# One decoder layer on one core: the seven products of a pair on four PSUM banks

## The chip, the core and the metric

The kernel runs on one core of one Trainium2 chip, in one launch. The metric is the device time in microseconds (us) of that core, as the median of several executions. In the profile PE is TensorE (the matrix engine), DVE is VectorE, ACT is ScalarE, POOL is GpSimd and SP is the engine that issues most of the DMAs. SBUF is the on-chip memory that all engines work in, PSUM the eight banks of 512 fp32 values per partition into which PE accumulates its products. Each engine executes its own instructions in the order in which the program has them; between engines they wait on semaphores.

## The reference, cut to what matters

One layer with a sequence of 1024 and a model width of 1024, all in float32:

```python
xn = rmsnorm(x, norm_mix_w[l])
proj = xn @ w_in[l]                       # 1024 x 4352
...                                       # two attentions on parts of proj, gates, merge
x = x + merged @ w_mix_out[l]
xn = rmsnorm(x, norm_ffn_w[l])
u = xn @ w_up                             # 1024 x 5632
c = conv_b + sum over j of shifted u * conv_w[j]    # causal, width 3
gate, val = split(c)                      # 2816 columns each
x = x + (silu(gate) * val) @ w_down
```

The change lies in two of these products: part of `xn @ w_in` (the projection stage) and all of `xn @ w_up` (the hidden stage).

## The kernel before, in words

**Numbers.** Every fp32 matrix is held as a high and a low part in a reduced type (fp32r). A product of two such matrices takes three matmuls for each 128-row step of the contraction: high by high, high by low, low by high. Splitting is one copy on ACT (the high part) and one subtraction on DVE (the low part).

**Pairs.** The weight columns are taken in pairs of 128-column blocks, and each pair is multiplied by a Strassen-like scheme with seven block products in place of eight. The activations (transposed, 1024 channels by 1024 positions) are cut into quarters: by channels (first and second 512) and by positions (first and second 512). From these come the right-hand operands `B11`, `B21`, `B22` and the differences `T1` to `T4`, made once for a stage. From the weights of the pair come the left-hand operands `A11`, `A12`, `A22` and the sums `S1` to `S4`, made for each pair: `sum_pair` (lines 86 to 99) loads two blocks by DMA (`raw`, `rv`) and computes the sums on POOL (lines 96 to 99, tiles `sf`), `split_pair` (lines 102 to 115) splits them (ACT line 110, DVE line 112). The tiles have names and a few buffers each: `wh`/`wl` (2 buffers) take `A11` and `A12` together, then `A22`; `sh`/`sl` take `S1` and `S2` together, then `S3` and `S4` together (2 buffers in the projection, 3 in the hidden stage); `sf` has 2 buffers. A buffer is written again when its readers are done.

**The seven products.** `product` (line 828, matmuls on lines 835 to 837) puts one block product of 12 matmuls into one PSUM bank. `P1 = A11 B11`, `P2 = A12 B21`, `P3 = S4 B22`, `P4 = A22 T4`, `P5 = S1 T1`, `P6 = S2 T2`, `P7 = S3 T3`. Each has a bank of its own out of eight that rotate (pools `psA` and `psF`). `recombine` (lines 389 to 402) then makes the four quarters of the result: ACT copies `P1` to SBUF (`s1`, line 395); seven additions on DVE, each with one operand in PSUM, make `c11 = P2 + s1` (396), `u2 = P6 + s1` (397), `u3 = P7 + u2` (398), `c22 = P5 + u3` (399), `u4 = P5 + u2` (400), `c12 = P3 + u4` (401), `c21 = u3 - P4` (402). `c11` and `c12` are the two halves of the first block's tile `us`, `c21` and `c22` those of the second's.

**Behind it.** In the projection (nine pairs after five plain blocks) POOL multiplies each `us` by the row scale `rstd` (line 385) and `keep` (lines 404 to 420) splits it and stores it to DRAM. In the hidden stage (22 pairs, j = 0 to 21) `conv` (lines 962 to 973) follows for each `us`: multiplication by `rstd` on POOL (line 965), bias and first tap on ACT (line 970), two more taps on DVE (971, 972). `glu` (lines 950 to 959) applies SiLU on ACT (957), multiplies gate and value on DVE (958) and stores the result to DRAM. During one pair the operands of the next two are made.

**The first pair of the hidden stage.** The row scale is not ready when it starts. PE sums the squares (line 158), POOL raises them to the power -1/2 (line 167, tile `rs`), and PE spreads the result over the columns (eight transposes, line 173), from where ACT copies it into `rstd` (line 907). Before these eight transposes stand the first two products of pair 1.

**Order.** A tile framework turns the program into one instruction list for each engine and puts in the semaphores. The order within each list is fixed when the kernel is built. PE takes pair by pair, product by product; DVE, ACT and POOL each take a mix of three kinds of work: recombining this pair, the convolution of the pair before, the operands of the pairs to come.

Of the kernel before, what the change touches and what calls it, by code (L numbers as in the profile page):

```python
# [13 lines left out]
ALU = mybir.AluOpType  # L14
# [3 lines left out]
P = 128  # L18
# [4 lines left out]
H2 = 512  # L23
DFF = 2816
NF = DFF // P
# [17 lines left out]
class Trunk:  # L43
# [206 lines left out]
    def project(self):  # L250


        nc, tc = self.nc, self.tc
# [3 lines left out]
        with ExitStack() as ctx:  # L257
            e = ctx.enter_context
            psA = self.psT = e(tc.tile_pool(name="psA", bufs=8, space=PSUM, reuse_waits="tile"))
# [8 lines left out]
            bank = lambda: self.tl(psA, [P, H2], "t")  # L268
# [11 lines left out]
            def diffs(k):  # L280

                (a, a2), (b, b2) = ([xr[r][:, hf * H2:(hf + 1) * H2] for hf in range(2)] for r in (k, k + 4))
                tt = nc.vector.tensor_tensor
                tt(a, a2, a, ALU.subtract)
                tt(a2, b2, a2, ALU.subtract)
                tt(b2, b2, a, ALU.subtract)
                tt(b, b2, b, ALU.subtract)

            def parts(k):
                for n, r in enumerate((k, k + 4)):  # L290
# [81 lines left out]
                     ("P6", "S2", "T2"), ("P4", "A22", "T4"))  # L372
            for j, ms in enumerate(self.pairs):
                w = self.next_w()
                pp = {}
                for name, a, b in (prods[i] for i in ((0, 1, 4, 2, 3, 5, 6) if j == 0 else (0, 1, 2, 5, 3, 4, 6))):
                    pp[name] = bank()
                    self.product(pp[name], w[a], b)
                us = [self.tl(tp, [P, T], "us", bufs=3) for _ in range(2)]
                self.recombine(pp, us, tp, 0)  # L380
                for m, u in zip(ms, us):
                    if self.kind[m] == "g":
                        nc.sync.dma_start(self.gd[m - 18], u)
                    else:
                        nc.gpsimd.tensor_tensor(u, u, self.rstd, ALU.mult)
                        self.keep(m, u, (tp, "hi"))
        self.uw = None

    def recombine(self, ps, us, tp, o):

        nc = self.nc
        c11, c12, c21, c22 = (us[w][:, o + hf * H2:o + (hf + 1) * H2] for w in range(2) for hf in range(2))
        s1, u2, u3, u4 = (self.tl(tp, [P, H2], n, bufs=1) for n in ("s1", "u2", "u3", "u4"))
        tt = nc.vector.tensor_tensor
        nc.scalar.copy(s1, ps["P1"])
        tt(c11, ps["P2"], s1, ALU.add)
        tt(u2, ps["P6"], s1, ALU.add)
        tt(u3, ps["P7"], u2, ALU.add)
        tt(c22, ps["P5"], u3, ALU.add)
        tt(u4, ps["P5"], u2, ALU.add)  # L400
        tt(c12, ps["P3"], u4, ALU.add)
        tt(c21, u3, ps["P4"], ALU.subtract)

    def keep(self, m, u, to):

# [397 lines left out]
    def operands(self, xt, xtp, xw, k):  # L803

        tt = self.nc.vector.tensor_tensor
        (b11, b12), (b21, b22) = ([xw[kc][:, hf * H2:(hf + 1) * H2] for hf in range(2)] for kc in (k, k + 4))

        def put(name, t):
            hi, lo = self.split(xt[name, k, "h"], xt[name, k, "l"], t)
            if name == "T13":  # L810
                self.B["T1", k], self.B["T3", k] = ((hi[:, c], lo[:, c]) for c in (slice(0, H2), slice(H2, T)))
            else:
                self.B[name, k] = hi, lo

        put("B11", b11)
        put("B21", b21)
        put("B22", b22)
        if k == 3:
            self.t42.append(xw[k + 4])
        t4, t2 = (self.t42[k][:, c] for c in (slice(0, H2), slice(H2, T)))  # L820

        tt(b11, b12, b11, ALU.subtract)
        tt(b12, b22, b12, ALU.subtract)
        put("T13", xw[k])
        tt(t2, b22, b11, ALU.subtract)
        tt(t4, t2, b21, ALU.subtract)

    def product(self, ps, a, b, ks=range(4), first=True, last=True, skip=False):

# [9 lines left out]
    def hidden(self, pair):  # L839
        nc, tc = self.nc, self.tc  # L840
        with ExitStack() as ctx:
            e = ctx.enter_context
            psF = e(tc.tile_pool(name="psF", bufs=8, space=PSUM, reuse_waits="tile"))
            self.psT = psF
            xc2 = e(tc.tile_pool(name="xc2", bufs=1, side="right", reuse_waits="tile"))
            self.uw = e(tc.tile_pool(name="uw", bufs=3, side="right", reuse_waits="tile"))
            prods = (("P1", "A11", "B11"), ("P2", "A12", "B21"), ("P5", "S1", "T1"), ("P7", "S3", "T3"),
                     ("P3", "S4", "B22"), ("P6", "S2", "T2"), ("P4", "A22", "T4"))
            with tc.high_priority(400):
                w0 = self.split_pair(*pair)  # L850
            ready = {}
            for j in range(NF):
                w, ps = ready.pop(j) if j else (w0, {})
                if j == 0:

                    for name, a, b in prods[:5]:
                        ps[name] = self.tl(psF, [P, H2], "t")
                        self.product(ps[name], w[a], b, range(3), last=False)
                    for k in range(4):
                        hi, lo = self.split(*(xc2.tile([P, T], F32R, name=f"T42_{k}{p}") for p in "hl"), self.t42[k])  # L860
                        self.B["T4", k], self.B["T2", k] = ((hi[:, c], lo[:, c]) for c in (slice(0, H2), slice(H2, T)))
                    self.tctx.close()
                    tp = e(tc.tile_pool(name="tp", bufs=2, side="right", reuse_waits="tile"))
                    ssq = self.tl(psF, [P, H2], "t")
                    for n, (name, a, b) in enumerate(prods[:5]):
                        self.product(ps[name], w[a], b, (3,), first=False)
                        if n == 4:
                            self.col_sums(ssq, [self.rstd], NB, 0)
                            with tc.high_priority(400):
                                rs = self.rstd_cols(ssq, 8, D)  # L870
                if j == NF - 1:

                    with tc.high_priority(50):
                        for k, r in enumerate(raw):
                            for hf in range(2):
                                h = self.tl(self.uw, [P, 2, H2], ("sh", "sl", "rv", "rv", "sh", "sl")[2 * k + hf], F32R, **({"bufs": 2} if k == 1 else {}))
                                self.hs[hf, k] = self.split(h[:, 0], h[:, 1], r[:, hf * H2:(hf + 1) * H2])
                        lo = self.lo
                for name, a, b in (prods[i] for i in ((0, 1, 2, 5, 3, 6, 4) if j == NF - 1 else (0, 1, 2, 5, 3, 4, 6) if j else range(7))):
                    if name not in ps:  # L880
                        ps[name] = self.tl(psF, [P, H2], "t")
                        self.product(ps[name], w[a], b)
                us = [self.tl(tp, [P, T + 2], "us", bufs=3) for _ in range(2)]
                if j == NF - 1:
                    self.defer.pop(0)(lo)
                    self.xctx2.close()
                    self.uw = None
                    self.open_down()
                    self.deep = True
                    with tc.high_priority(100):  # L890
                        self.ahead(2)
                self.recombine(ps, us, tp, 2)
                if j < NF - 1:

                    w, ps = ready[j + 1] = self.next_w(), {}
                    if j == NF - 2:
                        raw = [self.tl(self.sfp[0], [P, T], "t42", bufs=1)] + [self.tl(self.sfp[0], [P, T], "sf") for _ in range(2)]
                        for k, r in enumerate(raw):
                            nc.sync.dma_start(r, self.hd[k])
                    for name, a, b in prods[:2 if j == 0 else 0]:  # L900
                        ps[name] = self.tl(psF, [P, H2], "t")
                        self.product(ps[name], w[a], b)
                if j == 0:
                    for hf in range(2):
                        sp = self.tl(psF, [P, H2], "t")
                        self.spread(sp, rs, hf * 4)
                        nc.scalar.copy(self.rstd[:, hf * H2:(hf + 1) * H2], sp)

                for w in range(2):
                    f = lambda after=None, j=j, w=w, us=us: self.glu(j, w, us[w], tp, after)  # L910
                    if j + w < NF - 1:
                        f()
                    else:
                        self.defer.append(f)
# [296 lines left out]
```

## Time and profile before

| what | value |
|---|---|
| median of 3 runs | 1356.11 us (1355.26 to 1356.71) |
| the profiled execution | 1356.2 us, of which the span from first to last instruction is 1354.3 us |
| granted PE clock, mean | 0.996 of full speed |
| matmuls recorded | 6304 |

The page of the profile gives each engine's busy time. A group line has an engine, an operation, the tiles written and read, a count and a mean duration. In a timeline each row has the start and the duration in us, then engine, source line, operation, tiles, shape, and in brackets for how long the engine had been idle before it and what ended that. PE's matmuls overlap in their pipeline, so the rate of PE is read from the distance between two starts and not from the duration of one.

### The profile page before, as it was taken

To read this page: it belongs to the slowest core of one execution; us is meant where nothing else is said; L and a number is where in the kernel's file an instruction comes from. 1 tells how busy PE (TensorE), PEld (TensorE's weight loads), DVE (VectorE), ACT (ScalarE), POOL (GpSimd) and SP (SyncE) were. 2 spreads that over 40 slices of the span, in tenths; PEclk is the share of its full clock that TensorE was granted. 3 is DMA by queue.
4 is the path that set the end of the run, shared out by engine and by line. 5 is a ranking of instruction groups with operands and counts; after the bars stand their busy time and mean duration, and the time that the engine had idled before them with its cause. 6 is when DMAs were issued, how large, how long until landed. Compare 5 with 4: busy or idle time off the path is not lost.

```text
span 1354.3 us, 17160 instructions
## 1 busy us (share of the span) xinstructions
PE 1335.0 (99%) x6304; PEld 1103.6 (81%) x6304; DVE 1009.8 (75%) x1454; ACT 603.9 (45%) x942; POOL 483.1 (36%) x350
## 2 busy tenths in 40 slices
PE   7999999999999999999999999999999999999997
PEld 6888888888887777878888888888888888888886
DVE  8846775388898875355689888888888898986454
ACT  8422232376667664334444334433443345433343
POOL 0436651010102125741455565555555611231011
PEclk9999999999999999999999999999999999999999
DMA  6334443966554235334422222122212248651342
GB/s 255 140 113 164 143 156 114 272 174 175 156 133 144 77 116 219 117 119 136 166 82 88 71 91 94 62 79 93 93 63 83 92 141 311 215 177 64 94 134 85
DMA packets 62470, 179.50 MB, mean 133 GB/s; under 512 B 6833, under 2 KB 15153, under 8 KB 62385
## 3 DMA queue, kind: packets, MB, share of 16 engines
q1 hardware_dynamic: 50928, 160.98, 36.7%
q10 hardware_dynamic: 11456, 17.41, 3.5%
q8 instruction: 50, 0.82, 0.2%
q14 instruction: 36, 0.29, 0.1%
HBM read 129.61 MB, written 48.76 MB: 132 GB/s over the span
## 4 chain that ended last, share of the span: by engine, by line
PE 62%; DVE 17%; POOL 7%; issue 7%; DMA 4%; ACT 3%; POOLq 0%; DVEq 0%; SPq 0%; ACTq 0%
PE t L836 7%; PE t L837 7%; PE t L835 7%; POOL us L965 3%; PE y L996 3%; PE d L996 3%; PE sc L568 3%; PE g L150 2%; PE g L151 2%; DVE c L958 2%; PE g L152 2%; DVE wl L112 2%; DMA gr<-gd 2%; PE sc L151 2%; PE sc L152 2%
## 5 line engine op out<-in xcount | busy, mean ns | idle before, releaser
L970 ACT ACTIVATE c<-us,vecs 128x1024 f32<-128x1024 f32 x44 | 54.8, 1248 | 163.2 <-POOL us L965 160.0
L965 POOL TENSOR_TENSOR us<-us,rstd 128x1024 f32<-128x1024 f32 x42 | 100.7, 2414 | 52.8 <-DVE wl L131 34.3
L110 ACT CAST sh<-sf 128x1024 fp32r<-128x1024 f32 x62 | 64.9, 1051 | 106.2 <-POOL sf L97 61.8
L129 ACT CAST wh<-raw 128x1024 fp32r<-128x1024 f32 (+2 forms) x60 | 60.7, 1012 | 104.8 <-PE sc L151 33.1
L971 DVE SCALAR_TENSOR_TENSOR c<-us,vecs,c 128x1024 f32<-128x1024 f32 x44 | 67.1, 1527 | 51.9 <-ACT c L970 51.9
L131 DVE TENSOR_TENSOR wl<-raw,wh 128x1024 fp32r<-128x1024 f32 (+2 forms) x60 | 75.3, 1256 | 39.1 <-ACT wh L129 29.3
L96 POOL TENSOR_TENSOR sf<-rv 128x512 f32<-128x512 f32 x30 | 42.5, 1417 | 166.7 <-DMA rv<-in_w_up 73.2
L112 DVE TENSOR_TENSOR sl<-sf,sh 128x1024 fp32r<-128x1024 f32 x62 | 88.3, 1426 | 8.2 <-ACT sh L110 8.2
L167 POOL TENSOR_TENSOR rs<-ms,mhalf 128x8 f32<-128x8 f32 (+2 forms) x9 | 14.5, 1614 | 159.1 <-DVE ms L165 148.5
L150 PE MATMUL g<-xh,wh 128*128 128x512 f32 x176 | 70.7, 402 | 0.1
L152 PE MATMUL g<-xh,wl 128*128 128x512 f32 x176 | 70.4, 400 | 0.0
L151 PE MATMUL g<-xl,wh 128*128 128x512 f32 x176 | 70.4, 400 | 0.0
L98 POOL TENSOR_TENSOR sf<-raw,rv 128x512 f32<-128x512 f32 x30 | 41.6, 1386 | 59.9 <-DVE sl L112 59.9
L572 DVE CUSTOM_DVE_ANT_0 L<-sc,bias 128x128 f32<-128x128 f32 (+7 forms) x64 | 47.7, 752 | 17.4 <-PE sc L568 14.1
L551 POOL MEMSET aT<- 128x128 f32 x32 | 6.1, 204 | 152.0 <-PE t L597 101.6
L573 ACT ACTIVATE L<-L,sm 128x128 f32<-128x128 f32 (+7 forms) x64 | 49.6, 778 | 20.7 <-DVE sm L572 18.2
L97 POOL TENSOR_TENSOR sf<-sf,raw 128x512 f32<-128x512 f32 x31 | 58.0, 1870 | 1.6
L972 DVE SCALAR_TENSOR_TENSOR c<-us,vecs,c 128x1024 f32<-128x1024 f32 x44 | 56.2, 1279 | 0.6
L725 POOL TENSOR_TENSOR gr<-gr,rstd 128x1024 f32<-128x1024 f32 x16 | 39.4, 2467 | 41.4 <-DMA gr<-gd 41.2
L112 DVE TENSOR_TENSOR wl<-raw,wh 128x1024 fp32r<-128x1024 f32 (+1 forms) x35 | 52.8, 1508 | 0.1
L151 PE MATMUL sc<-ml,wh 128*128 128x512 f32 x128 | 50.1, 391 | 0.6 <-DVE ml L746 0.6
L568 PE MATMUL sc<-u,u 128*128 128x512 f32 (+2 forms) x192 | 49.8, 359 | 0.1
(444 smaller groups left out, 4351.4 us busy)
## 6 DMA issues: line engine op xcount, KB each, us to landing
u<-qd SPq DMA_DIRECT2D x72, 256.0 KB, 6.1
raw<-in_w_down SPq DMA_DIRECT2D x27, 512.0 KB, 3.7
raw<-in_w_in SPq DMA_DIRECT2D x25, 512.0 KB, 4.4
hr<-hd SPq DMA_DIRECT2D x50, 256.0 KB, 5.3
raw<-in_w_up SPq DMA_DIRECT2D x23, 512.0 KB, 3.6
hd<-c SPq DMA_DIRECT2D x22, 512.0 KB, 2.8
rv<-in_w_up SPq DMA_DIRECT2D x21, 512.0 KB, 3.5
gr<-gd SPq DMA_DIRECT2D x16, 512.0 KB, 3.6
```

Of the source, the lines that this page charges most:

```text
L112: nc.vector.tensor_tensor(lo, src, hi.bitcast(F32), ALU.subtract)
L131: self.lo = (eng or nc.vector).tensor_tensor(wl, raw, wh.bitcast(F32), ALU.subtract)
L150: nc.tensor.matmul(ps, wh[:, kc + o, :], ah, start=first and n == 0, stop=False)
L151: nc.tensor.matmul(ps, wh[:, kc + o, :], al, start=False, stop=False)
L152: nc.tensor.matmul(ps, wl[:, kc + o, :], ah, start=False, stop=last and n == len(kcs) - 1)
L568: nc.tensor.matmul(sc[:, lo + n0:lo + n1], qs, k[c][part][:, n0:n1], start=part == 0, stop=part == 1)
L835: nc.tensor.matmul(ps, ah[:, k, :], bh, start=first and n == 0, stop=False, skip_group_check=skip)
L836: nc.tensor.matmul(ps, ah[:, k, :], bl, start=False, stop=False, skip_group_check=skip)
L837: nc.tensor.matmul(ps, al[:, k, :], bh, start=False, stop=last and n == len(ks) - 1, skip_group_check=skip)
L965: i = (nc.vector if m % NF == 0 else nc.gpsimd).tensor_tensor(us[:, 2:], us[:, 2:], self.rstd, ALU.mult)
L971: nc.vector.scalar_tensor_tensor(c, us[:, 1:T + 1], cw[1], c, ALU.mult, ALU.add)
L996: nc.tensor.matmul(ps, v[:, n, :], x, start=n == i == 0, stop=n == len(js) - 1 and i == 2)
```

## The change

The pairs after the first of each stage go through a new function, `seven`, with four PSUM banks in place of seven and the products in another order. Three products are accumulated onto a bank that already holds another one, once that one has been read: `P2` onto `P1`, `P4` onto `P7`, `P3` onto `P5`. For this the sign of `T4` is turned, so that `P4` is added.

```diff
-                tt(b, b2, b, ALU.subtract)
+                tt(b, b, b2, ALU.subtract)
...
                 us = [self.tl(tp, [P, T], "us", bufs=3) for _ in range(2)]
-                self.recombine(pp, us, tp, 0)
+                if j == 0:
+                    pp = {}
+                    for name, a, b in (prods[i] for i in (0, 1, 4, 2, 3, 5, 6)):
+                        pp[name] = bank()
+                        self.product(pp[name], w[a], b)
+                    self.recombine(pp, us, tp, 0)
+                else:
+                    self.seven(psA, w, us, tp, 0)
...
-        tt(c21, u3, ps["P4"], ALU.subtract)
+        tt(c21, ps["P4"], u3, ALU.add)
+
+    def seven(self, pool, w, us, tp, o):
+
+        nc = self.nc
+        c11, c12, c21, c22 = (us[r][:, o + hf * H2:o + (hf + 1) * H2] for r in range(2) for hf in range(2))
+        s1, u2, u3 = (self.tl(tp, [P, H2], n, bufs=1) for n in ("s1", "u2", "u3"))
+        tt = nc.vector.tensor_tensor
+        a, b, c, d = (self.tl(pool, [P, H2], "t") for _ in range(4))
+        self.product(a, w["A11"], "B11", skip=True)
+        nc.scalar.copy(s1, a)
+        self.product(b, w["S2"], "T2")
+        tt(u2, b, s1, ALU.add)
+        self.product(c, w["S3"], "T3", skip=True)
+        tt(u3, c, u2, ALU.add)
+        self.product(d, w["S1"], "T1", skip=True)
+        tt(c22, d, u3, ALU.add)
+        self.product(a, w["A12"], "B21", first=False, skip=True)
+        nc.scalar.copy(c11, a)
+        self.product(c, w["A22"], "T4", first=False, skip=True)
+        tt(c21, c, u2, ALU.add)
+        self.product(d, w["S4"], "B22", first=False, skip=True)
+        tt(c12, d, u2, ALU.add)
...
-        tt(t4, t2, b21, ALU.subtract)
+        tt(t4, b21, t2, ALU.subtract)
...
-                for name, a, b in (prods[i] for i in ((0, 1, 2, 5, 3, 6, 4) if j == NF - 1 else (0, 1, 2, 5, 3, 4, 6) if j else range(7))):
...
+                if j == 0:
+                    for name, a, b in prods:
+                        if name not in ps:
+                            ps[name] = self.tl(psF, [P, H2], "t")
+                            self.product(ps[name], w[a], b)
+                    self.recombine(ps, us, tp, 2)
+                else:
+                    self.seven(psF, w, us, tp, 2)
...
-                    for name, a, b in prods[:2 if j == 0 else 0]:
-                        ps[name] = self.tl(psF, [P, H2], "t")
-                        self.product(ps[name], w[a], b)
```

The last three removed lines are those that put the first two products of pair 1 ahead of the eight transposes in the hidden stage.

In the built kernel the matmuls of a pair stay 84. DVE loses two additions per pair (`c11` and `u4`), ACT gains one copy (`c11`). DVE's order in pair j of the hidden stage is: `u2`, gate times value of pair j-1, `u3`, `c22`, low part of `S3`/`S4` for pair j+1, low part of `A11`/`A12` for j+1, `c21`, low part of `A22` for j+1, `c12`, low part of `S1`/`S2` for j+2, and the four taps of the convolution of pair j; then `u2` of pair j+1. ACT's order is: `s1`, SiLU of j-1, high parts of `S3`/`S4` and of `A11`/`A12` for j+1, `c11`, high part of `A22` for j+1, high part of `S1`/`S2` for j+2, first taps of pair j (first block, then second). POOL's order is: the sums `S3`, `S4` for j+2, `us` of pair j times `rstd` (second block, then first), the sums `S1`, `S2` for j+3.

More of the change, by code (lines that the diff above doesn't have):

```diff
@@ L374, in project @@
                 w = self.next_w()
[L375 to L378, printed above, removed]
                 us = [self.tl(tp, [P, T], "us", bufs=3) for _ in range(2)]
-                self.recombine(pp, us, tp, 0)
+                if j == 0:
[6 more added lines that the diff above has]
+                    self.seven(psA, w, us, tp, 0)
                 for m, u in zip(ms, us):
@@ L878, in hidden @@
                         lo = self.lo
-                for name, a, b in (prods[i] for i in ((0, 1, 2, 5, 3, 6, 4) if j == NF - 1 else (0, 1, 2, 5, 3, 4, 6) if j else range(7))):
-                    if name not in ps:
-                        ps[name] = self.tl(psF, [P, H2], "t")
-                        self.product(ps[name], w[a], b)
                 us = [self.tl(tp, [P, T + 2], "us", bufs=3) for _ in range(2)]
+                if j == 0:
[6 more added lines that the diff above has]
+                    self.seven(psF, w, us, tp, 2)
                 if j == NF - 1:
@@ L891, in hidden @@
                         self.ahead(2)
-                self.recombine(ps, us, tp, 2)
                 if j < NF - 1:
@@ L899, in hidden @@
                             nc.sync.dma_start(r, self.hd[k])
-                    for name, a, b in prods[:2 if j == 0 else 0]:
-                        ps[name] = self.tl(psF, [P, H2], "t")
-                        self.product(ps[name], w[a], b)
                 if j == 0:
```

## The prediction

> **What bounds the kernel now.** I read the page first, then a table by stretches, then the timelines of four engines over one pair of the hidden stage.
>
> ```profile
> span 1354.3 us, 17160 instructions
> PE 1335.0 (99%) x6304; PEld 1103.6 (81%) x6304; DVE 1009.8 (75%) x1454; ACT 603.9 (45%) x942; POOL 483.1 (36%) x350
> ```
> ```profile
> core 0: us, PE busy (x) PEld busy (x) DVE busy (x) ACT busy (x) POOL busy (x), PEclk, DMA share, GB/s
> 726.20:1092.10 365.90, 365.57 (x1598) 298.65 (x1597) 313.32 (x304) 142.84 (x154) 205.09 (x151) 1.00 0.25 82
> 86.00:242.00 156.00, 156.00 (x690) 129.23 (x689) 106.31 (x109) 44.24 (x51) 76.86 (x46) 1.00 0.41 150
> 699.60:703.00 3.40, 3.40 (x9) 2.23 (x8) 3.40 (x4) 2.83 (x4) 0.10 (x1) 0.50 0.00 0
> ```
>
> PE is busy everywhere. The first stretch is pairs 2 to 20 of the hidden stage, with DVE at 313 of 366 us; the second is pairs 1 to 8 of the projection, with DVE at 106 of 156.
>
> ```profile
> 726.22 0.39 PE L835 MATMUL t<-B_0h,wh 128*128 128x512 f32 x1
> ...
> 840.55 0.39 PE L835 MATMUL t<-B_0h,wh 128*128 128x512 f32 x1
> 840.78 0.39 PE L836 MATMUL t<-B_0l,wh 128*128 128x512 f32 x1
> 841.23 0.51 PE L837 MATMUL t<-B_0h,wl 128*128 128x512 f32 x1
> ...
> 1092.03 0.39 PE L835 MATMUL t<-B_0h,wh 128*128 128x512 f32 x1
> ```
>
> Undisturbed matmuls start 0.227 us apart (840.55 to 840.78), so a product of 12 takes 2.72 and a pair of 84 takes 19.03. Pair 2 starts at 726.22 and pair 21 at 1092.03: 365.8 / 19 = 19.25 for a pair. The 0.22 more is one wait: at 841.23 PE comes 0.22 late, for the low part of `A11`. The next rows show who sets that.
>
> ```profile
> 839.30 1.88 DVE L112 TENSOR_TENSOR wl<-raw,wh 128x1024 fp32r<-128x1024 f32 x1
> 841.10 2.30 DVE L958 TENSOR_TENSOR c<-c,c 128x1024 f32<-128x1024 f32 x1
> ...
> 843.92 1.21 DVE L112 TENSOR_TENSOR sl<-sf,sh 128x1024 fp32r<-128x1024 f32 x1
> 845.05 0.68 DVE L398 TENSOR_TENSOR u<-t,u 128x512 f32<-128x512 f32 x1
> 845.77 0.69 DVE L399 TENSOR_TENSOR us<-t,u 128x512 f32<-128x512 f32 x1
> 846.38 0.68 DVE L400 TENSOR_TENSOR u<-t,u 128x512 f32<-128x512 f32 x1
> ...
> 847.77 1.22 DVE L112 TENSOR_TENSOR sl<-sf,sh 128x1024 fp32r<-128x1024 f32 x1
> ...
> 852.16 1.73 DVE L971 SCALAR_TENSOR_TENSOR c<-us,vecs,c 128x1024 f32<-128x1024 f32 x1 [2.58 <-ACT c L970]
> 853.80 0.68 DVE L112 TENSOR_TENSOR wl<-rv,wh 128x512 fp32r<-128x512 f32 x1
> 854.41 1.28 DVE L972 SCALAR_TENSOR_TENSOR c<-us,vecs,c 128x1024 f32<-128x1024 f32 x1
> 855.60 1.28 DVE L971 SCALAR_TENSOR_TENSOR c<-us,vecs,c 128x1024 f32<-128x1024 f32 x1
> ...
> 1091.81 1.21 DVE L958 TENSOR_TENSOR c<-c,c 128x1024 f32<-128x1024 f32 x1
> ```
> ```profile
> 838.80 1.29 POOL L96 TENSOR_TENSOR sf<-rv 128x512 f32<-128x512 f32 x1 [5.42 <-DVE c L972]
> ...
> 840.17 2.14 POOL L97 TENSOR_TENSOR sf<-sf,raw 128x512 f32<-128x512 f32 x1
> 845.21 1.29 POOL L98 TENSOR_TENSOR sf<-raw,rv 128x512 f32<-128x512 f32 x1 [2.90 <-DVE sl L112]
> 846.47 1.29 POOL L99 TENSOR_TENSOR sf<-raw,sf 128x512 f32<-128x512 f32 x1
> ...
> 847.93 4.87 POOL L965 TENSOR_TENSOR us<-us,rstd 128x1024 f32<-128x1024 f32 x2
> ...
> 1109.62 2.00 POOL L965 TENSOR_TENSOR us<-us,rstd 128x1024 f32<-128x1024 f32 x1 [4.47 <-DVE sl L756]
> ```
> ```profile
> 850.87 1.25 ACT L970 ACTIVATE c<-us,vecs 128x1024 f32<-128x1024 f32 x1 [7.48 <-POOL us L965]
> 852.03 0.60 ACT L110 CAST wh<-rv 128x512 fp32r<-128x512 f32 x1
> ...
> 853.99 0.56 ACT L395 COPY s<-t 128x512 f32<-128x512 f32 x1
> ...
> 857.62 1.04 ACT L110 CAST sh<-sf 128x1024 fp32r<-128x1024 f32 x1
> ```
>
> Two readings. First, a loop beside PE: `us` times `rstd` on POOL, first tap on ACT, taps on DVE, recombination on DVE, and again. None of these rows waits for PE. The recombination is a pair late, which eight rotating banks allow. Second, DVE and POOL exclude each other when DVE reads two SBUF tensors. Line 958 takes 1.21 alone (1091.81) and 2.30 where POOL's line 97 runs until 842.31. That one takes 2.14 against 1.29 of its sister at 846.47, because DVE's row from 839.30 ends at 841.18, 1.0 after its start. The two multiplications take 4.87 against twice 2.00, because DVE's row from 847.77 ends at 848.99. Who waits goes next. The additions at 845.05 to 846.38, with one operand in PSUM, keep their 0.68 beside POOL. So DVE work on SBUF and all POOL work form one queue.
>
> **The change part by part.** Two additions a pair leave DVE: at 0.61 from start to start (845.77 to 846.38) that is 1.2 us. DVE is not what PE waits for by its total, so this counts only inside the loop. The copy of `c11` on ACT (0.56 as at 853.99) lies in ACT's idle time. The sign and operand order of `T4` cost nothing: as many operations of the same shape, once a stage.
>
> The new wait. `T4`'s product goes onto `c` only when `u3` has read it; `u3` stands on DVE behind the whole convolution of the pair before, and behind the waiting matmul stands all of PE. Nominally that product starts 5 products, 13.6 us, into the pair. Before, the same lateness was covered by the spare banks. I follow the loop from the start of `u3` in pair j (time 0) in the order of the built program, with starts of successors from the rows above.
>
> `c22` at 0.7, low part of `S3`/`S4` 1.3 to 2.5. This frees `sf`, and POOL wants line 98 at 2.6. But DVE's next instruction, the low part of `A11`/`A12` (`A12`'s product, which held the buffer, is done), has begun at 2.45 and holds the path to 3.6; line 98 ends at 4.9. `c21` (after the product that started at about 0.75 and ended at 3.6) needs no path. The low part of `A22`, waiting since 4.3, goes next, to 5.5; line 99 ends at 6.75, a small fill comes behind it (846.47 to 847.93 is 0.17 more than the 1.29), and the multiplication of the second block runs to 8.9. PE ends the pair at about 6.3. `c12` follows to 7.05, the cast of `S1`/`S2` (their buffer is held by `S4` until then) ends at 7.45, and the low part behind it waits for POOL, 8.9 to 10.0. The first block's multiplication, kept back by that, ends at 12.0. First tap on ACT to 13.3. On DVE four taps at 1.2 each with POOL's line 97 (1.29) between them: 19.4. `u2` to 20.0, gate times value (1.15) to 21.1: there `u3` of pair j+1 starts. The loop is 21.1 us, and PE's 19.03 is shorter, so PE waits some 2 us in each pair at `T4`'s product.
>
> The full loop runs for j = 2 to 18, since POOL makes no more `S1`, `S2` after that: 17 x (21.1 - 19.25) = 31.5; pair 19 has the loop without lines 96 and 97, 19.8: 0.5. Together +32. Bounds for the loop: the four waits for the path (1.1, 0.6, 1.1, 1.3) are the part I only infer. With two of them gone it is 19.4, with none PE's 19.03; with one more POOL operation of 1.29 in the convolution 22.4. I take 21.1, as all four follow from who is queued first by margins of 0.15 to 0.6.
>
> The transposes.
>
> ```profile
> 696.59 1.95 PE L158 MATMUL t<-ones,rstd 128*128 128x1 f32 x16
> ...
> 706.26 0.39 PE L835 MATMUL t<-B_0h,wh 128*128 128x512 f32 x1
> ...
> 707.27 2.65 POOL L167 TENSOR_TENSOR rs<-ms,mhalf 128x8 f32<-128x8 f32 x1
> ...
> 708.98 0.39 PE L835 MATMUL t<-B_0h,wh 128*128 128x512 f32 x1
> ...
> 711.70 1.03 PE L173 MATMUL t<-ident,rs 128*128 128x128 f32 x8
> ...
> 712.49 0.48 PE L835 MATMUL t<-T_0h,sh 128*128 128x512 f32 x1
> ```
>
> Pair 1's first two products (706.26 to 711.70) covered the wait for `rs`, ready at 709.92. Without them PE is idle from 706.26 to 709.95: +3.7. Pair 1 then starts at 710.75. Its clock may fall: at 699.60 to 703.00 it was 0.50, after sixteen one-column matmuls, and 3.4 us held 9 matmuls where 15 fit. Such a stretch costs up to 1.7; I take 1.3, total +5.0 (3.7 to 5.4). The Trainium skill, TensorE: Matmul & The Clock Gate, section Why this matters for your kernels, tells to leave no PE-idle gaps of over about 3 us, or the clock halves. By it this gap would cost the 1.7, and the 2 us waits in the pairs nothing.
>
> The projection: DVE has 50 us idle there, and `u3` does not stand behind a convolution, only behind one low part and its POOL multiplication. That chain is at most 0.7 + 2.9 (4.87 - 2.00) + 1.05 + 1.2 = 5.9 after the pair's end, then `u2`, so `u3` runs as soon as `T3`'s product is there, 8.2 us into the pair, against 13.6. 0, at most +2 in pair 1, whose `u2` follows the old recombination. If that cover went, each of eight pairs would pay its lateness.
>
> SP: in the hidden stage the load of `rv` follows the low part of `A22` and takes 3.5 in the page's DMA list.
>
> ```profile
> rv<-in_w_up SPq DMA_DIRECT2D x21, 512.0 KB, 3.5
> ```
>
> Here that is 5.5 + 3.6 = 9.1, before POOL asks for it at 12.0. No cost; a landing after 12.0 would only move lines 96 and 97 further into the taps. `wh` comes free after the fifth product instead of the second; cast (1.04) and low part (1.9 at most) fit into the two products left, 5.4.
>
> Sum: 1356.2 (the profiled execution; the median is 0.1 lower) + 32 + 5 = 1393 us.
>
> **The rivals.** (1) Part of the waits for the path is absent, since POOL and DVE meet at other moments: loop 19.5 to 20.3, +4 to +18 and the 5, 1365 to 1380. For it: the times above are sums of twenty steps. Against: the orders are fixed and the loop has little slack. (2) PE stays the bound. Then 19.03 a pair, 19 x 0.22 = 4.2 gained, 5 lost: 1357, no change. It needs all four waits gone. (3) The other side, faster: DVE's relief of 1.2 us and earlier operands remove PE's 0.22 a pair, and `rs` comes 3.7 us sooner, so that the transposes cost nothing: 1356.2 - 4.2 = 1352. Against it: the row of line 167 stands behind the same instructions as before, line 97 among them. (4) The waits of 2 us halve the clock each time. A slow stretch loses 1.7 us of PE; while the loop is longer than PE's 20.7 it hides, but added to the loop it gives 22.8: 17 x 3.55 + 5, 1421; half of that, 1407. For it: the 0.50 above came without a long idle time. Against: PE is idle for 2 us of each 21 only.
>
> **How the numbers follow.** The forecast has 0.66, with a range of its own of 1380 to 1404 (loop 20.4 to 21.7). Rival 1 has 0.14, rival 2 0.08, rival 3 0.05, rival 4 0.07. A change of under 0.2% (2.7 us) is no change here. Slower: 0.66 + 0.14 + 0.07 = 0.87; same 0.08; faster 0.05. The range 1360 to 1406 leaves out rivals 2 and 3 and most of 4.
>
> **What would show it.** Right: PE's starts leave a gap of 1.5 to 2.5 us at the sixth product of pairs 3 to 19 (the first matmul of `T4` by `A22`), ended by DVE's `u3`; the pairs start about 21 us apart; PE's idle time in the stage rises to over 20 us; a gap of 3.7 us before the transposes, ended by line 167; none in the projection. Wrong: pairs 19.0 to 19.3 apart, the sixth product on time, or a wait at the weights (low part of `A11`) in place of `u3`.

## The result and the profile after

The changed kernel takes 1393.27 us (median of 5 runs, 1391.61 to 1394.73) where the kernel before takes 1356.11: a ratio of 1.0273, 95% interval 1.0259 to 1.0287. The prediction was 1393.0. The profiled execution has a span of 1391.5 us against 1354.3, 37.2 more. That is the number to take apart, for a total that is right may be made of parts that are not.

The head of the page of the changed kernel, as shown of before:

```profile
span 1391.5 us, 17119 instructions
PE 1341.3 (96%) x6304; PEld 1104.9 (79%) x6304; DVE 981.6 (71%) x1396; ACT 621.4 (45%) x971; POOL 497.4 (36%) x350
```

PE has as many matmuls and is busy 6 us longer, so 31 of the 37 us are idle time of PE. DVE does 28 us less and the kernel is slower. To place the loss, take the start of the same matmul (by its number in PE's order) in both traces; the difference grows like this:

| stretch | predicted, us | measured, us |
|---|---|---|
| start and projection (all of it at pair 2, but 0.3) | 0 | +4.4 |
| attention and mix | 0 | +3.3 |
| transposes and first products of pair 1 | +5 | +5.3 |
| hidden stage, pairs 1 to 21 | +32 | +22.3 |
| first products of the down projection | 0 | +2.1 |
| rest | 0 | -0.2 |
| sum | +37 | +37.2 |

The large term is two thirds of what was forecast, and 9.8 us in three places were not forecast at all. That the total is right to the microsecond is luck: these errors cancel.

Lines after the new function stand 25 higher than before: 835 is 860, 965 is 990, 971 and 972 are 996 and 997, 958 is 983. The list of waits of the changed kernel in 760 to 1060 us (total, times, longest), and two rows of PE's timeline with the wait behind them in brackets:

```profile
POOL sf L98 <- DVE sl L112: 74.4, 14, 5.3
...
DVE c L996 <- ACT c L995: 47.6, 15, 3.2
...
PE t L860 <- DVE u L419: 16.0, 14, 1.2
```
```profile
856.56 0.50 PE L860 MATMUL t<-T_0h,wh 128*128 128x512 f32 x1 [1.17 <-DVE u L419]
877.04 0.50 PE L860 MATMUL t<-T_0h,wh 128*128 128x512 f32 x1 [1.14 <-DVE u L419]
```

Line 419 is `u3`; the waiting row is the first matmul of `T4` by `A22`, sixth product of the pair, once in each pair from 2 to 19 (one pair sooner than predicted). The two rows are a pair apart: 20.48 us. From start to start PE's gap is 1.5 us, 1.3 beyond a matmul's pitch. Now the loop on DVE and POOL, from one `u3` to the next, in the timelines of the two engines:

```profile
855.83 0.68 DVE L419 TENSOR_TENSOR u<-t,u 128x512 f32<-128x512 f32 x1
...
857.22 1.22 DVE L112 TENSOR_TENSOR sl<-sf,sh 128x1024 fp32r<-128x1024 f32 x1
858.35 1.22 DVE L112 TENSOR_TENSOR wl<-raw,wh 128x1024 fp32r<-128x1024 f32 x1
...
860.23 1.05 DVE L112 TENSOR_TENSOR wl<-rv,wh 128x512 fp32r<-128x512 f32 x1
...
863.25 2.25 DVE L112 TENSOR_TENSOR sl<-sf,sh 128x1024 fp32r<-128x1024 f32 x1 [0.22 <-ACT sh L110]
868.68 3.58 DVE L996 SCALAR_TENSOR_TENSOR c<-us,vecs,c 128x1024 f32<-128x1024 f32 x2 [3.17 <-ACT c L995]
872.19 2.47 DVE L997 SCALAR_TENSOR_TENSOR c<-us,vecs,c 128x1024 f32<-128x1024 f32 x2
874.58 0.68 DVE L417 TENSOR_TENSOR u<-t,s 128x512 f32<-128x512 f32 x1
...
876.31 0.68 DVE L419 TENSOR_TENSOR u<-t,u 128x512 f32<-128x512 f32 x1
```
```profile
858.52 2.21 POOL L98 TENSOR_TENSOR sf<-raw,rv 128x512 f32<-128x512 f32 x1 [5.32 <-DVE sl L112]
860.69 1.74 POOL L99 TENSOR_TENSOR sf<-raw,sf 128x512 f32<-128x512 f32 x1
...
862.42 4.94 POOL L990 TENSOR_TENSOR us<-us,rstd 128x1024 f32<-128x1024 f32 x2
867.33 1.29 POOL L96 TENSOR_TENSOR sf<-rv 128x512 f32<-128x512 f32 x1
868.69 1.30 POOL L97 TENSOR_TENSOR sf<-sf,raw 128x512 f32<-128x512 f32 x1
```

The four predicted waits for the shared path are there: line 98 takes 2.21 instead of 1.3 behind the low part begun at 858.35; the low part of `A22` takes 1.05 instead of 0.68; the low part of `S1`/`S2` takes 2.25 instead of 1.2, between the two multiplications; the two first taps take 3.58 instead of 2.5, since line 97 runs from 868.69 to 869.99.

The idle time before the transposes, in the list of waits, and the clock (third number from the end) behind it, in windows of 3 us:

```profile
PE t L173 <- POOL rs L167: 3.6, 1, 3.6
```
```profile
714.50:717.50 3.00, 0.00 (x0) 0.00 (x0) 2.90 (x4) 1.56 (x2) 3.00 (x2) 0.98 0.57 175
717.50:720.50 3.00, 2.82 (x11) 2.63 (x12) 3.00 (x5) 1.17 (x2) 3.00 (x3) 0.50 0.01 3
```

And what had not been foreseen, in pair 2 of the projection:

```profile
PE t L862 <- DVE sl L112: 1.8, 1, 1.8
```
```profile
106.69 4.77 POOL L388 TENSOR_TENSOR us<-us,rstd 128x1024 f32<-128x1024 f32 x2
...
110.23 2.31 DVE L440 SCALAR_TENSOR_TENSOR us<-us,hi 128x1024 fp32r<-128x1024 f32 x1 [4.06 <-ACT hi L439]
112.46 1.21 DVE L112 TENSOR_TENSOR sl<-sf,sh 128x1024 fp32r<-128x1024 f32 x1
```

PE waits at the third product, `T3` by `S3`, for the low part of `S3`/`S4`. That part stands on DVE behind the low part of a kept pair (line 440). This one waits, by way of its high part on ACT (line 439), for POOL's multiplication, and then takes 2.31 beside it.

### The profile page after: what moved, and what is told of

It reads as the page before. It is cut to its first block, busy times and chain, and to the rows that moved or that the text cites. A ratio compares the mean times of both kernels' runs of the same rounds, so it can differ in the third digit from the quotient of the medians.

```text
span 1391.5 us, 17119 instructions
## 1 busy us (share of the span) xinstructions
PE 1341.3 (96%) x6304; PEld 1104.9 (79%) x6304; DVE 981.6 (71%) x1396; ACT 621.4 (45%) x971; POOL 497.4 (36%) x350
## 4 chain that ended last, share of the span: by engine, by line
PE 48%; POOL 14%; DVE 13%; issue 11%; DMA 3%; ACT 3%; SPq 0%; POOLq 0%; DVEq 0%; ACTq 0%
POOL us L990 5%; PE t L862 4%; PE t L860 4%; PE t L861 4%; PE y L1021 3%; PE d L1021 3%; POOL sf L98 3%; PE sc L593 3%; POOL sf L99 2%; DMA gr<-gd 2%; DVE c L997 2%; DVE sl L112 2%; POOL gr L750 2%; PE g L150 2%; DVE c L996 2%
## 5 line engine op out<-in xcount | busy, mean ns | idle before, releaser
L996 DVE SCALAR_TENSOR_TENSOR c<-us,vecs,c 128x1024 f32<-128x1024 f32 x44 | 75.8, 1757 | 63.3 <-ACT c L995 63.3
L112 DVE TENSOR_TENSOR sl<-sf,sh 128x1024 fp32r<-128x1024 f32 x62 | 105.6, 1706 | 12.9 <-ACT sh L110 12.8
L98 POOL TENSOR_TENSOR sf<-raw,rv 128x512 f32<-128x512 f32 x30 | 58.7, 1957 | 112.0 <-DVE sl L112 112.0
L597 DVE CUSTOM_DVE_ANT_0 L<-sc,bias 128x128 f32<-128x128 f32 (+7 forms) x64 | 47.8, 753 | 20.4 <-PE sc L593 14.0
L997 DVE SCALAR_TENSOR_TENSOR c<-us,vecs,c 128x1024 f32<-128x1024 f32 x44 | 55.5, 1297 | 0.0
L982 ACT ACTIVATE c<-c 128x1024 f32<-128x1024 f32 x22 | 23.4, 1063 | 68.9 <-DVE c L997 68.9
L99 POOL TENSOR_TENSOR sf<-raw,sf 128x512 f32<-128x512 f32 x31 | 51.5, 1660 | 0.2
L110 ACT CAST wh<-raw 128x1024 fp32r<-128x1024 f32 (+1 forms) x35 | 35.0, 999 | 33.5 <-PE t L861 18.2
```

Of the source, the lines that this page charges most:

```text
L98: tt(sb[:, 0], g[:, 0], v[:, 0], ALU.subtract)
L99: tt(sb[:, 1], g[:, 1], sa[:, 1], ALU.subtract)
L110: nc.scalar.copy(hi, src)
L112: nc.vector.tensor_tensor(lo, src, hi.bitcast(F32), ALU.subtract)
L996: nc.vector.scalar_tensor_tensor(c, us[:, 1:T + 1], cw[1], c, ALU.mult, ALU.add)
L997: nc.vector.scalar_tensor_tensor(c, us[:, 0:T], cw[0], c, ALU.mult, ALU.add)
```

## The experiments

Two readings of the steady pairs were to be told apart. One: PE waits because `T4`'s product now needs `u3`; make the product free, and PE is free. The other, on which the sum rested: DVE, POOL and ACT go round in 20.5 us whatever PE does, and the wait for `u3` is only where that shows. Differences below are to the changed kernel's 1393.3 unless another kernel is named. The kernel before, run again beside each set of these runs, took 1356.2 to 1356.9, so a difference under 1 us between sets says nothing.

**T4 on a bank of its own** (five banks a pair).

```
-        self.product(c, w["A22"], "T4", first=False, skip=True)
-        tt(c21, c, u2, ALU.add)
+        e = self.tl(pool, [P, H2], "t")
+        self.product(e, w["A22"], "T4")
+        tt(c21, e, u3, ALU.add)
```

> Edit: T4's product gets a bank of its own (five banks a pair), so it waits for no u3; order of products and of VectorE's, ScalarE's and GpSimd's instructions as in the changed kernel. Theory (a loop of VectorE, GpSimd and ScalarE of 20.5 us sets the pair, and PE's wait only shows it): pairs stay 20.4 to 20.5 us apart, the gap moves to the seventh product (S4 by B22 waits for c22), once 1.9 us gained, 1391.5 (1389 to 1393.5). Rival (it is the wait for u3 at the sixth product that costs, as the prediction's front edge of the step reads): the pairs fall to 19.0 to 19.3, about 20 us gained, 1371 (1369 to 1375).

Measured: 1389.28, 4.0 less; pairs 20.45 apart. The list of waits (760 to 1060 us), line 421 being `c22`:

```profile
PE t L861 <- DVE us L421: 14.3, 13, 1.1
```

The wait for `u3` is gone, a wait as long has come one product later, and the pair is as long as it was. Of the 4.0, some 2 came once in the hidden stage, as expected, and 2.1 at the down projection, whose first matmul no longer waits.

**T4 and S4 on banks of their own** (six a pair; `u4` comes back).

```
         tt(c22, d, u3, ALU.add)
+        tt(u4, d, u2, ALU.add)
...
-        self.product(d, w["S4"], "B22", first=False, skip=True)
-        tt(c12, d, u2, ALU.add)
+        f = self.tl(pool, [P, H2], "t")
+        self.product(f, w["S4"], "B22")
+        tt(c12, f, u4, ALU.add)
```

> Edit: T4's and S4's products both get banks of their own (six a pair), which brings back the addition u4 on VectorE (0.61 us from start to start); orders else as in the changed kernel. PE then waits for no recombination of its own pair or of the one before. Theory (the loop beside PE): pairs 21.1 us apart (20.5 and 0.6), the wait moves to the low part of A11, and the time is longer than the changed kernel's although a wait of PE is gone: 1401 (1397 to 1404). Rival (the wait for u3 is the cost): pairs 19.0 to 19.3, 1371 (1369 to 1375).

Measured: 1401.33, 8.1 more; pairs 21.04 apart.

```profile
PE t L866 <- DVE wl L112: 19.5, 13, 1.5
```

This is the run that decides. No product waits for an addition of DVE any more, and the kernel is slower by 0.6 us a pair, the one addition that the loop has got. PE now waits for the low part of `A11`/`A12`, because that is what the loop hands over late.

**u2 and u3 earlier on DVE**, by priority: `u3` ahead of the gate's multiplication, `u2` ahead of the last tap.

```
+        with self.tc.high_priority(60):
+            tt(u2, b, s1, ALU.add)
...
+        with self.tc.high_priority(60):
+            tt(u3, c, u2, ALU.add)
```

> Edit: u2 and u3 get priority in the chained products; on VectorE u3 then stands ahead of the gate's multiplication of the pair before and u2 ahead of the last tap, one instruction earlier each. Theory (loop beside PE, the same instructions in another order): pairs stay 20.4 to 20.5 apart, the gap moves behind the sixth product, at most 1.2 us gained once, 1392 (1389 to 1394). Rival (the place of u3 on VectorE is what costs): the gap falls from 1.5 to 0.3, pairs 19.3 apart, 1373 (1370 to 1377).

Measured: 1387.07, 6.2 less, below the expected range; pairs 20.29 apart. The loop theory holds in the main: the change is worth 0.2 a pair and not the rival's 1.2. But PE's wait did not move behind the sixth product as the theory had it, and the 0.2 had not been seen. In the changed kernel `c22` reads `u3` and starts 0.78 behind it, where unrelated additions follow each other at 0.61; here the multiplication comes between the two, 0.60 behind `u3`. That this pause is the 0.2 is read from the rows; no run tried it alone.

**Convolution in PSUM.** The accumulators `c` go into the four banks that the chained products leave free (those of the last two pairs stay in SBUF), and SiLU writes its result to a tile in SBUF; orders on all engines stay.

```
-            psF = e(tc.tile_pool(name="psF", bufs=8, space=PSUM, reuse_waits="tile"))
+            psF = e(tc.tile_pool(name="psF", bufs=4, space=PSUM, reuse_waits="tile"))
...
+                    self.psC = e(tc.tile_pool(name="psC", bufs=2, space=PSUM, reuse_waits="tile"))
...
-        c = self.tl(self.cpl, [P, T], "c")
+        c = self.tl(self.cpl if m % NF >= NF - 2 else self.psC, [P, T], "c")
```

> Edit: from pair 0 on, the convolution's accumulators (first tap, the four taps of VectorE, the input of the gate) lie in PSUM, in the four banks that the chained products leave free; the sums, multiplications and orders are as in the changed kernel. Theory (VectorE reading two SBUF tensors and GpSimd exclude each other, with one operand in PSUM they don't): the first tap of a pair takes 1.3 us where it took 2.4 (it waited for line 97), so the loop falls from 20.5 to about 19.3, PE's pitch or near it, 17 pairs by 1.1 to 1.25: 1373 (1369 to 1378). Rival (no such exclusion, the long rows have another cause, or PSUM accumulators are slower): the taps keep their times or grow, 1393 or more.

Measured: 1365.45, 27.8 less; all pairs 19.04 apart, PE's own pitch, and no wait of PE left in 760 to 1060. DVE's and POOL's timelines of that run:

```profile
869.31 1.23 DVE L112 TENSOR_TENSOR wl<-raw,wh 128x1024 fp32r<-128x1024 f32 x1 [1.24 <-ACT wh L110]
...
874.81 3.00 DVE L112 TENSOR_TENSOR sl<-sf,sh 128x1024 fp32r<-128x1024 f32 x1 [0.22 <-ACT sh L110]
878.00 2.48 DVE L1002 SCALAR_TENSOR_TENSOR c<-us,vecs,c 128x1024 f32<-128x1024 f32 x2 [0.20 <-ACT c L1001]
880.39 2.48 DVE L1003 SCALAR_TENSOR_TENSOR c<-us,vecs,c 128x1024 f32<-128x1024 f32 x2
```
```profile
868.15 1.30 POOL L98 TENSOR_TENSOR sf<-raw,rv 128x512 f32<-128x512 f32 x1 [5.30 <-DVE sl L112]
...
874.73 2.00 POOL L996 TENSOR_TENSOR us<-us,rstd 128x1024 f32<-128x1024 f32 x1 [0.41 <-DVE us L427]
877.94 1.30 POOL L96 TENSOR_TENSOR sf<-rv 128x512 f32<-128x512 f32 x1 [1.21 <-DVE sl L112]
879.31 1.29 POOL L97 TENSOR_TENSOR sf<-sf,raw 128x512 f32<-128x512 f32 x1
```

The taps at 878.00 take 2.48 for two although POOL's lines 96 and 97 run the whole time: with one operand in PSUM nothing waits. The low part at 874.81, two SBUF inputs, still takes 3.00 beside POOL's row of 874.73. So it is the operands that decide, as the prediction had inferred. The Trainium skill, GPSIMD Engine Reference, section 1. Specifications, names this sharing, as contention of GpSimd with VectorE instructions that have two SBUF inputs; the rows agree, and show it as waiting for each other's whole instruction.

The gain was larger than the 20 expected, and the time lies below the expected range. Line 98 takes 1.30 here: the low part at 869.31 waited for ACT's cast, and that for PE, so that POOL got the path first. So one of the other waits went too, and PE sets the pace. From pair 1 on the hidden stage now takes 4.2 us less than in the kernel before. The kernel as a whole still takes 9 more, because 7.9 are lost ahead of the hidden stage and 6.4 at the transposes.

**Three buffers for `sf`**, so that line 98 needs no low part of the pair before; POOL then has lines 96, 98, 97, 99 in a row. (To make room, `u4` of `recombine` shares a tile with `s1`.)

```
+    def sums_tile(self):
...
+            self.ns += 1
+            if self.ns % 3 == 1:
+                return self.tl(third, [P, 2, 4, P], "sf")
...
+        return self.tl(self.sfp[0], [P, 2, 4, P], self.sfp[1])
```

> Edit: from pair 0 on the raw sums sf rotate over three buffers, so GpSimd's line 98 no longer waits for the low part of S3 and S4 of the pair before (the longest wait of GpSimd in the list of waits, 5.3 us a pair); GpSimd then has lines 96, 98, 97, 99 one behind the other, beside the taps. Theory (VectorE's work on two SBUF tensors and GpSimd's work form one queue, and the pair is the sum of that queue, 19.2, and of the PSUM additions that no GpSimd work overlaps): the two instructions only move along the queue, pairs 20.4 to 21.9, 1393 to 1417, no gain. Rival (the wait of line 98 closes the loop): pairs 19.2 to 19.5, 1373 (1370 to 1378).

Measured: 1405.84, 12.6 more; pairs 21.02 apart. DVE's and POOL's timelines:

```profile
873.24 4.23 DVE L1009 SCALAR_TENSOR_TENSOR c<-us,vecs,c 128x1024 f32<-128x1024 f32 x2 [0.24 <-ACT c L1008]
877.39 4.55 DVE L1010 SCALAR_TENSOR_TENSOR c<-us,vecs,c 128x1024 f32<-128x1024 f32 x2
```
```profile
872.29 1.87 POOL L96 TENSOR_TENSOR sf<-rv 128x512 f32<-128x512 f32 x1 [0.37 <-DMA rv<-in_w_up]
874.12 2.27 POOL L98 TENSOR_TENSOR sf<-raw,rv 128x512 f32<-128x512 f32 x1
876.35 2.27 POOL L97 TENSOR_TENSOR sf<-sf,raw 128x512 f32<-128x512 f32 x1
878.71 2.16 POOL L99 TENSOR_TENSOR sf<-raw,sf 128x512 f32<-128x512 f32 x1
```

The longest wait of POOL in the list, 5.3 us a pair, was taken away, and the kernel lost. The two engines alternate, tap by sum, and the four taps take 8.7 instead of 6.0 (868.68 to 874.66 in the changed kernel). The time is inside the range of the queue theory.

**Pair 1's first two products ahead of the transposes again.**

```
                     w, ps = ready[j + 1] = self.next_w(), {}
+                    if j == 0:
+                        ab = self.first_two(psF, w)
```

> Edit: pair 1's products A11 by B11 and S2 by T2 are issued ahead of the eight transposes again, all else as in the changed kernel. Theory (the step of the transposes: 3.7 us idle until line 167 has written rs, and a clock at half behind it): the idle time of 4.0 us before the transposes falls under 0.5, the clock stays at 1.00, and the time is 5 us shorter, 1388 (1387 to 1389.5). Rival (the two products only stand in another place, and the loop beside PE, which starts with pair 1, sets the end of the stage whatever PE does before it): less than 1.5 us is gained, 1392 to 1394.

Measured: 1389.13, 4.1 less: the time that the theory gave, but not for its reason. The idle time before the transposes is gone, and two other waits stand in pairs 1 and 2, in the list of waits (722 to 762 us; line 424 is `u3`, line 426 `c22`); behind the second the clock falls:

```profile
PE t L865 <- DVE us L426: 2.7, 1, 2.7
PE t L865 <- DVE u L424: 2.4, 1, 2.4
```
```profile
728.50:731.50 3.00, 0.30 (x2) 0.00 (x0) 3.00 (x5) 2.94 (x4) 1.75 (x1) 1.00 0.00 0
731.50:734.50 3.00, 2.98 (x13) 2.49 (x14) 3.00 (x2) 0.16 (x2) 2.80 (x4) 1.00 0.20 83
...
748.00:751.00 3.00, 0.81 (x4) 0.34 (x2) 3.00 (x4) 3.00 (x4) 0.00 (x0) 0.99 0.00 0
751.00:754.00 3.00, 2.78 (x7) 2.21 (x8) 2.90 (x4) 0.09 (x1) 0.83 (x1) 0.50 0.43 175
```

From the transposes to the end of pair 2, by matmul numbers, this run loses 7.5 us on the kernel before, the changed one 6.7. So the rival's mechanism fits, though not its time: DVE's additions, not PE, decide when pair 2 is through. The 4.8 us between the two spans (1391.5 and 1386.7) lie elsewhere: 2.1 at the down projection, 1.8 in the projection (where the code is the same: scatter between executions, see the last section), 1.4 in the steady pairs, 0.4 in the attention, less the 0.8 and 0.2 in the rest.

**Chained products in the hidden stage alone; in the projection alone.** The first puts back the kernel before's loop over the projection's pairs, the second its hidden stage, without a line of their own to show.

> Edit: the chained products stay in the hidden stage, the projection is as in the kernel before. Theory (the changed kernel loses 2.7 to 4.1 us at pair 2 of the projection, where the low part of S3 and S4 stands on VectorE behind the low part of a kept pair, and up to 3.3 in the attention, whose blocks start later and in another phase): 1387 (1385 to 1391), no gap over 1 us in the projection. Rival (the prediction's term for the projection, nothing): 1393, no difference beyond 1 us.

> Edit: the chained products stand in the projection alone, the hidden stage is as in the kernel before. Theory (2.7 to 4.1 us at pair 2 of the projection, up to 3.3 in the attention, nothing behind it): 1361 (1358 to 1364), pairs of the hidden stage 19.25 apart. Rival (projection costs nothing): 1356 to 1357.

Measured: 1387.54 and 1363.29. With the projection as before, PE runs through pair 2 (108 to 117 us) without a pause:

```profile
108.00:117.00 9.00, 9.00 (x41) 7.47 (x40) 3.11 (x4) 2.95 (x4) 6.02 (x4) 1.00 0.48 168
```

and the attention loses nothing (from +0.1 to -0.7 against before). With the chained products there alone, pair 2 loses 4.4 and the attention another 2.0, and the hidden stage ends within 0.2 us of where that puts it. So the attention's loss follows from the projection. It consists of a few gaps of 0.8 to 1.5 us in the changed kernel; what each of them waits for was not tried. Its size isn't fixed: over the eight runs that have the chained products in the projection, pair 2 loses 2.7 to 4.8 and the attention 0.5 to 5.3, and the hidden stage starts 5.5 to 7.9 late. In the three runs with the projection as before it starts 0.6 to 1.0 early.

**Towards a faster kernel.** Projection as before, convolution in PSUM and the first two products ahead, together:

> Edit: three edits together: chained products in the hidden stage alone, the convolution's accumulators in PSUM, pair 1's first two products ahead of the transposes. Theory (the loss of the projection goes, the steady pairs run at PE's 19.04, 4 us less than the kernel before had; but pair 1 keeps the two waits of 2.6 and 2.9 behind u3 and c22 that the run with the first two products alone showed, 7.5 us to the third pair, since u3 of pair 1 stands on VectorE behind the convolution of pair 0): 1356.5 - 0.5 + 7.5 - 4 = 1359.5 (1357 to 1361). Rival (the first lap was late through the old, longer loop, and those waits go too): 1352 (1350 to 1354).

Measured: 1357.79, a ratio of 1.0010 to the kernel before, interval 1.0000 to 1.0019: no difference. That the time fits the theory is luck, for neither part does. From the transposes to the end of pair 2 the run lost 1.2 us, not 7.5: there the rival was right. The steady pairs ran at 19.31, not 19.04. With the same order on DVE as the run with the convolution in PSUM, the low part of `A11`/`A12` came 0.17 ahead of line 98 here, and that row is long again:

```profile
876.89 1.22 DVE L112 TENSOR_TENSOR wl<-raw,wh 128x1024 fp32r<-128x1024 f32 x1
...
877.06 2.21 POOL L98 TENSOR_TENSOR sf<-raw,rv 128x512 f32<-128x512 f32 x1 [5.30 <-DVE sl L112]
```

The same three edits with the priority for `u2` and `u3`:

> Edit: as the three edits together, and u2 and u3 of the chained products get priority, by which both of pair 1 stand ahead of pair 0's taps on VectorE, and u3 of the later pairs ahead of the gate's multiplication. Theory (u3 behind the convolution of pair 0 is what pair 1 waits for): no gap over 1 us in pairs 1 to 19, pairs 19.04 apart, 1352.5 (1351 to 1354), shorter than the kernel before by 0.3%. Rival (pair 1 waits for something else in that first lap, the transposes' copy or the weights): as without the priority, 1357 to 1361.

Measured: 1353.65 (11 runs, 1352.77 to 1354.19), a ratio of 0.9979 to the kernel before, interval 0.9970 to 0.9988. The time is inside the range of the theory. Pairs 19.04 to 19.15 apart, no gap over 1 us in the hidden stage. This is the fastest of all kernels here, by 2.6 us. PE's waits of 0.22 in each of 19 pairs had cost the kernel before 4.2; of these the steady pairs win back 3.1.

## Why the prediction was right, and where not

**The loop as the bound: right**, and the runs show it from both sides. Taking the wait for `u3` away did not change the pair (20.45). With no wait left for an addition, but one more addition in the loop, the pair grew by that addition (21.04). Taking four taps and the gate off the path let the pair fall to PE's own 19.04, or to 19.31 where line 98 still came second.

**The price of the loop: too high.** The step that was mis-sized is the sum of the twenty steps, 21.1 against 20.48. Set side by side, in us after `u3`:

| event | predicted | measured |
|---|---|---|
| line 98 ends | 4.9 | 4.90 |
| low part of `A22` ends | 5.5 | 5.45 |
| second block's multiplication starts | 6.9 | 6.59 |
| first block's multiplication ends | 12.0 | 11.53 |
| first tap on DVE starts | 13.3 | 12.85 |
| `u2` starts | 19.4 | 18.75 |
| next `u3` starts | 21.1 | 20.48 |

Every wait was placed rightly; the sum is 0.3 too long at the end of line 99 and the small fill behind it (line 99 ends at 862.43, the multiplications start at 862.42, so the fill costs nothing), 0.15 in the two multiplications, 0.2 in the four taps with line 97. It is the same kind of error in three places, always adding: full durations and pauses where successors overlap by a little. Times 17 this is 10.5; the stage came out 9.7 below the 32. The loop ended at the lower edge of the forecast's own range, 20.4.

**The transposes: the size right, the sum not.** The idle time (4.0 from start to start) and the clock of 0.50 behind it came as worked out, 5.3 in all. That it hit so closely is partly luck: the seven runs with this gap lose 4.0 to 6.7 here, depending on how long the clock stays at 0.50. But the term stood in the sum as if undoing it would give it back; the run with the two products ahead lost as much in pairs 1 and 2.

**The projection: wrong.** The step that failed is "0, at most +2 in pair 1". It followed the chain that sets `u3`, and asked nothing of the weights that the same queue carries. On DVE the low part of `S3`/`S4` stands behind the kept pair's, and PE waited 1.8 us for it; with the projection as before that wait is gone. Why the built order puts it there is argued and not shown: `S4` has become the last product, so the buffer of `S3`/`S4` comes free only with the pair. The note that the weights fit had been worked out for `wh` in the hidden stage alone.

**Attention and down projection: left out.** The 3.3 and 2.1 were not in the sum, nor in a rival. At the down projection, the first product of the next stage waits for the last `c12` (1.9 us, line 427). A late `c12` is not enough for that: with the first two products ahead it also ends 1.9 us behind the start of that product (1145.44 and 1143.56), and nothing waits. Which bank the product gets may make the difference; that was not tried.

**The clock.** Eighteen gaps of 1.5 us cost nothing beside their length, as forecast against rival 4; the granted clock of the steady stretch is 1.00:

```profile
757.00:1085.00 328.00, 309.71 (x1346) 251.19 (x1345) 254.02 (x225) 129.17 (x145) 184.16 (x129) 1.00 0.23 77
```

## What to carry to other kernels

When a change turns buffers into waits, first find out whether the loop that fills them is longer than the engine that will wait; removing the wait then gives nothing, and each instruction added to the loop costs its full length per turn. Where two engines share a path, count the time on that path as one queue, and ask which operand can be moved off it: here the banks that the change had freed were worth 28 us as accumulators for VectorE. Against the kernel that used them as spare banks for PE that is 2.6 us in the best combination and nothing without the priority for `u2` and `u3`. A stage's weights and results wait in the same queue, so a chain followed for one of them must be followed for the others too.

## What the hardware showed unexpectedly

The clock after a short idle time differs between executions of the same instructions. In pair 2 of the projection the changed kernel and the run with the convolution in PSUM have nearly the same two gaps, the longer of 2.2 us from start to start. One runs at half clock behind it and loses 4.1 us at that place, the other loses 2.7. The run with the first two products ahead shows both in one execution: full speed behind a gap of 3.1 us, 0.50 behind one of 2.8.

The times at which the traces record a change of clock show what decides. Within each of the twelve runs they lie a multiple of 3.41 us apart (in the changed kernel 113.24, 116.66, 707.16, 710.58, 717.40 and 720.82), and each stretch at 0.50 between the first and the last matmuls lasts 3.41 or 6.83 us. Cut by these steps, the place in pair 2 looks like this, first in the changed kernel, then in the other:

```profile
109.83:113.24 3.41, 1.70 (x7) 0.77 (x5) 3.01 (x2) 1.79 (x3) 1.63 (x1) 1.00 0.65 268
113.24:116.66 3.42, 2.93 (x7) 2.35 (x8) 1.03 (x2) 0.00 (x0) 2.50 (x2) 0.50 0.49 198
```
```profile
108.89:112.30 3.41, 2.15 (x9) 1.13 (x7) 2.59 (x2) 2.20 (x3) 2.04 (x1) 1.00 0.53 219
112.30:115.71 3.41, 2.50 (x11) 2.09 (x12) 1.45 (x2) 0.00 (x0) 2.48 (x2) 1.00 0.62 247
```

In the changed kernel nearly all of the idle time falls into one step, in which PE is busy for 1.70 of 3.41 us, and the next step runs at 0.50. In the other run the end of a step, at 112.30, divides the gap. In the run with the first two products ahead the gap of 3.1 us is divided (1.75 and 2.35 busy), while most of that of 2.8 lies in one step (1.27 busy). Over all steps of the twelve traces, PE busy for 1.6 us or less was always followed by 0.50, and for more than 1.8 never, save where one-column matmuls or transposes stood in the step; between 1.6 and 1.8 both occur. So in these runs the limit is about half a step. The loop's idle time of 1.3 us a pair cannot take half a step wherever it falls; a wait of 2 us, as predicted, could have (it leaves 1.4 of 3.41), so rival 4 was nearer than the prediction gave it. A gap of 2.8 us was enough for half clock, and so was one of 2.25 us in front of the down projection in the run with the chained products in the hidden stage alone (0.50 from 1140.90 on).

The Trainium skill, TensorE: Matmul & The Clock Gate, section What's actually happening, has the activity watched in windows that run freely, which makes it a matter of where a gap falls, and gives 3.4 us for a window. The traces agree, with 3.41. The limit of about 3 us that the prediction quotes does not hold here, as the gaps of 2.8 and 2.25 us show.

The loop has more than one stable phase. The same order of instructions went round in 19.31 us in one kernel and kept up with PE's 19.04 in another, as the low part of `A11`/`A12` came just ahead of line 98 or behind it. The rows show which came first; no run held the one fixed and moved the other.
